# Hybrid attention/SSD layer on one core: new transfer prices and a longer search in the planner that orders the instructions

## The chip, the cores and the metric

The kernel runs on one core of a Trainium2 chip, alone. The metric is the device time of one execution in microseconds (us); smaller is better. A core has a matrix engine (PE), a vector engine (DVE), a scalar engine (ACT), a general engine (POOL) and a queue engine (SP) that issues most of the transfers (DMA). Each engine takes its instructions in the order in which they stand in its own queue and waits where an input or a buffer is not ready; the engines meet through semaphores.

## What is computed

One layer (DEPTH = 1) of a diffusion backbone on 512 latent tokens of width 1024 with 256 context tokens, in float32:

```python
cq_x, ckv_x, kr_x, z_x, xbc_x, dt_x = in_split(
    modulate(rms_norm(x, mix_pre_norm[l]), mod_x[0], mod_x[1]) @ w_in[l])
...
attn_x = latent_attention(q_nope_x, q_rope_x,
                          jnp.concatenate([k_nope_c, k_nope_x], axis=1),
                          jnp.concatenate([kr_c, k_rope_x], axis=1),
                          jnp.concatenate([v_c, v_x], axis=1))
...
y_x = ssd_output(st_xf[0], st_xf[1]) + flip(ssd_output(st_xb[0], st_xb[1]))
ssd_x = ssd_finish(y_x, xs_x, z_x, ssd_d[l], ssd_norm[l])
mix_x = jnp.concatenate([attn_x, ssd_x], axis=-1) @ w_out[l]
x = x + mod_x[2] * rms_norm(mix_x, mix_post_norm[l])
ffn_x = conv_glu(modulate(rms_norm(x, ffn_pre_norm[l]), mod_x[3], mod_x[4]),
                 w_up[l], ffn_conv_w[l], ffn_conv_b[l], w_down[l])
x = x + mod_x[5] * rms_norm(ffn_x, ffn_post_norm[l])
```

There are 16 attention heads (64 plain and 32 rotary dimensions, keys and values from a low-rank latent of width 256) and 16 SSD heads (chunks of 128 tokens, both directions).

## The kernel before

The source `build` writes the whole layer once, straight through, in an order that is easy to read. Matrices are cut into blocks of 128 rows and at most 512 columns. A float32 operand is split into a high and a low part (`split`: L498 on ACT makes the high part, L499 on DVE the difference), and a product is three PE passes over these parts. Storage in the on-chip memory is 53 blocks of 128 partitions by 1024 words; each tensor (`t4`, `t2`) takes a piece of a block. In the profile every such piece is called `block`, and every matmul result `banks`.

The stages of the profile, by the lines that dominate them:

- 0 to 150 us: modulation vectors, the norm of x, and the input projections (L686, and L759 in `gemm_T`).
- 150 to 520 us: the rest of the input projection (`rest_of_in`), the SSD (`ssd`, L1034 to L1091) and, beside them, the attention of eight pairs of heads.
- 520 to 610 us: the output projection L1326 on the rows `wout`, with the norms after it; DVE meanwhile forms more modulation values from the rows `wmod` (L587).
- 610 to 850 us: the gated MLP up (L759); 850 to 975 us: the MLP down (L1519) and the last norm.

Two places of the middle stage matter here.

*The operands of a pair of heads* (`project`, called "the projection of a pair" below). The product of the keys of both heads (in `gemm_T`, L759) lands in one bank, and is split into the block `kx[0]`: rows 0 to 63 belong to the first head, rows 64 to 127 to the second. Line L1176 copies rows 64 to 127 into `kx[1]` by DMA, block to block. Only when that copy has landed may L1181 copy the rotary keys over the same rows 64 to 127 of `kx[0]`. The queries go the same way (L1179, L1180), and the context keys `kcj` (L1176, L1182). These are 56 transfers of 128 KB and 32 of 256 KB. The first score matmul of the pair (`scores`, L1203) needs them all. `scores` goes on with a maximum on DVE (L1205), an exponential on ACT (L1207), transposes on PE (L1219) with splits (L498, L499), and the weighted sum of values (L1231), which DVE takes up in L1257.

*The norm of the key latent* (`latent("wckv", ...)` in `rest_of_in`). PE sums squares against a column of ones (L845, six products). DVE scales the sums (L847); `rsqrt` takes a power on POOL (L522) and refines it on DVE (L523, L527, L528, L529), on tensors of 128x6. PE then spreads the six values over rows (L535, six products), DVE multiplies the latent by them (L855, twice), and the next products reuse the bank (L759).

The order in which instructions stand on each engine is not that of the source. `program` traces `build` once, and `plan` decides the order and which piece gets which block. `plan` prices each instruction (`price`), finds what depends on what (`dependences`), and plays a list schedule in which transfers share one queue (`Graph.schedule`; a reader of a transfer waits `DMA_WAIT + DMA_ALONE * cost` after its turn in that queue). Then it repeats rounds: it places the pieces in blocks by the start and end times of the round before, takes an older piece's block only where that piece ends `MARGIN` (2500 ns) earlier, adds the waits that shared blocks bring, and schedules again. The plan with the smallest modelled end is kept; its order becomes the program's.

Of the kernel before, what the change touches and what calls it, by code (L numbers as in the profile page):

```python
# [86 lines left out]
UNITS, EDGE, MARGIN = 212, 180, 2500  # L87
# [7 lines left out]
class Memory:  # L95
# [3 lines left out]
    def __init__(self, pool, plan=None):  # L99
        self.pool, self.plan, self.pieces, self.blocks = pool, plan, [], {}  # L100
# [48 lines left out]
         ("Pool", "Activation"): 75, ("Pool", "DVE"): 74, ("Pool", "PE"): 149, ("Pool", "Pool"): 102}  # L149

AHEAD = 40000
DMA_START, DMA_WAIT, DMA_AHEAD, DMA_ALONE, DMA_WORDS = 650, 910, 3000, 0.8, 5000


def engine_of(x):
    return str(x.engine).split(".")[-1]
# [5 lines left out]
def price(x):  # L162

    ops = [(v.bass_ap.tensor.name, list(v.ap), v) for l in (x.outs, x.ins) for v in l if hasattr(v, "bass_ap")]
    size = lambda o: math.prod(c for _, c in o[1][1:])
    e, n = engine_of(x), max(map(size, ops))
    chip = all(not o[0].startswith("banks") for o in ops)
    kind = type(x).__name__
    if "DMA" in kind:
        words = any(len(v.bass_ap.ap) > 1 and v.bass_ap.ap[-1][0] != 1 for v in x.outs if hasattr(v, "bass_ap"))  # L170
        return DMA_WORDS if words else size(ops[0]) * ops[0][1][0][1] * 4 / 360
    if e == "PE":
        if ops[1][2].dtype == mybir.dt.float32r:
            return size(ops[1]) / (2.4 if size(ops[1]) >= 256 else 1.2) + (13 if ops[1][1][0][1] > 64 else 100)
        return max(107, size(ops[1]) / 1.2) if x.is_transpose else max(213, size(ops[1]) / 0.6)
    if "Memset" in kind:
        return 35 + 0.83 * n
    if e == "Activation":
        return 72 + (43 if chip else 0) + 93 * (len(ops) - 2) + 0.833 * n
    if e == "Pool":  # L180
        return 150 + (1.66 if any(not s for o in ops for s, c in o[1][1:] if c > 1) else 2.1) * n
    if "Reciprocal" in kind:
        return 69 + 6.25 * n
    if "TensorScalar" in kind and chip and sum(size(o) > 1 for o in ops[1:]) < 2:
        return 69 + 0.52 * n
    return (130 if len(ops) == 4 else 69) + 1.04 * n
# [192 lines left out]
        return found  # L379


def plan(ins, pieces, hints, units, rounds=16):

# [16 lines left out]
                    preds[i].update(last)  # L402
    opens, shared = {u[0] for u in users.values()}, [ports(x) for x in ins]
    _, _, start, end = Graph(preds, eng, dma, cost, share, tables, urgent, opens, shared).best()
    found = None
    for _ in range(rounds):
        held, types = [(-1, -1e9, [])] * units, [None] * (units // 4)
        inst, before = [((), -1e9)] * (units // 4), [((), -1e9)] * (units // 4)
        full, places = [set(p) for p in preds], []
        for t, (n, type_), at in pieces:  # L410
            u = users[t]
            s0, s1 = min(start[i] for i in u), max(end[i] for i in u)
            able, free, due = [], {}, {}
            for o in range(0, units, STEP[n]):
                b = o // 4
                if (o + n - 1) // 4 == b:
                    h = held[o : o + n] if types[b] == type_ else held[b * 4 : b * 4 + 4]
                    if all(v[0] < at for v in h):
                        able.append(o)
                        free[o], due[o] = max(max(v[1] for v in h), (before if types[b] == type_ else inst)[b][1]), h  # L420

            fit = [o for o in able if free[o] + MARGIN <= s0]
            fit = [o for o in fit if (o >= EDGE) == (n < 3)] or fit
            if fit:
                o = max(fit, key=lambda o: sum(v[1] for v in due[o]) / len(due[o]))
            else:
                if not able:
                    break
                o = min(able, key=free.get)
            b = o // 4  # L430
            new = types[b] != type_
            if new:
                types[b], before[b], inst[b] = type_, inst[b], ((), -1e9)
            inst[b] = (*inst[b][0], *u), max(inst[b][1], s1)
            for i in u:
                full[i].update(before[b][0])
                for v in due[o]:
                    full[i].update(v[2])
            held[o : o + n] = [(max(u), s1, u)] * n
            places.append((o, new))  # L440
        if len(places) < len(pieces):
            continue
        took, order, start, end = Graph(full, eng, dma, cost, share, tables, urgent, opens, shared).best()
        if found is None or took < found[0]:
            found = took, places, order
    return found


# [1179 lines left out]
def program(arrays, dbg_shapes=None, **kw):  # L1628

    try:  # L1630
        trace(arrays, None, dbg_shapes, **kw)
    except Traced as t:
        tiles, hints, ins = t.args
    return trace(arrays, plan(ins, tiles, hints, UNITS), dbg_shapes, **kw)
# [9 lines left out]
```

## Time and profile before

| | |
|---|---|
| median of 3 runs | 976.13 us (975.1 to 976.65) |
| the profiled execution's own time | 976.79 us |
| span of its profile, first to last instruction | 975.0 us |
| PE busy | 953.7 us (98%), 5157 records |
| DVE, ACT, POOL busy | 680.0 (70%), 504.7 (52%), 184.4 us (19%) |
| mean granted PE clock | 0.995 of full |
| DMA | 122.94 MB, mean 126 GB/s |

The profile is one execution. "Busy" of PE counts overlapping matmuls once. A wait row names an instruction group, what it waited for, the total, how often, and the longest. A window row gives, for a stretch of the span, its length and the busy time of PE, its weight loads (PEld), DVE, ACT and POOL with the number of instructions in brackets, then the granted PE clock, the share of time in which the 16 DMA engines were busy, and the GB/s that they moved. `SPq` rows are transfers that SP issues. L numbers are lines of the kernel before.

### The profile page before, as it was taken

Reading aid. Unit: us, or ns where it says so; the run is one execution under the profiler, and the core shown is the slowest. Engines: PE = TensorE matmul, PEld = TensorE weight load, DVE = VectorE, ACT = ScalarE, POOL = GpSimd, SP = SyncE. Lnnn points to the kernel's source line nnn. Section 1 sums busy time; section 2 is a strip of 40 time slices with the busy share of each in tenths; the row PEclk is TensorE's granted clock in tenths of the full one; section 3 lists DMA queues with packets and bytes.
Section 4 is the critical chain, followed back from the end, with each engine's and each line's share of the span. In section 5 each row is a group of like instructions: output and inputs, shape, how many; then the busy total and the mean of one; then the engine's idle time right before and its main releaser. Section 6 shows DMA issues by size and latency. Waiting matters only on the chain.

```text
span 975.0 us, 14205 instructions
## 1 busy us (share of the span) xinstructions
PE 953.7 (98%) x5157; PEld 813.6 (83%) x5157; DVE 680.0 (70%) x1151; ACT 504.7 (52%) x1004; POOL 184.4 (19%) x187
## 2 busy tenths in 40 slices
PE   8999999999999999999899999999999999999997
PEld 7888888888878987888798888988888888878885
DVE  6999886999999987767789966735254342695214
ACT  4554337567579787787787026633142231662001
POOL 0002202657694535111010001000000000000000
PEclk9999999999999999999899999999999999999999
DMA  9924102012321351524839876231323203347321
GB/s 349 402 94 130 44 22 82 19 66 74 95 60 55 100 153 45 133 74 110 234 138 335 248 205 216 87 108 54 140 85 132 87 33 108 98 155 241 82 84 65
DMA packets 48037, 122.94 MB, mean 126 GB/s; under 512 B 8400, under 2 KB 11552, under 8 KB 47968
## 3 DMA queue, kind: packets, MB, share of 16 engines
q1 hardware_dynamic: 45424, 120.89, 38.6%
q10 hardware_dynamic: 2544, 1.15, 0.5%
q8 instruction: 41, 0.67, 0.3%
q14 instruction: 28, 0.23, 0.1%
HBM read 99.82 MB, written 6.46 MB: 109 GB/s over the span
## 4 chain that ended last, share of the span: by engine, by line
PE 80%; DVE 5%; DMA 3%; ACT 2%; issue 1%; POOL 0%; SPq 0%; DVEq 0%; ACTq 0%; POOLq 0%
PE banks L759 38%; PE banks L1519 12%; PE banks L1326 9%; PE banks L1203 5%; PE banks L1231 3%; PE banks L1219 3%; DVE block L499 2%; DMA block<-block 2%; PE banks L1135 1%; PE banks L686 1%; PE banks L1039 1%; PE banks L1084 1%; PE banks L1076 1%; DVE smalls L1205 1%; PE banks L808 1%
## 5 line engine op out<-in xcount | busy, mean ns | idle before, releaser
L759 PE MATMUL banks<-block,block 128*128 128x512 f32 (+1 forms) x2132 | 443.2, 360 | 1.1 <-DVE block L855 1.1
L759 PEld LDWEIGHTS banks<-block,block 128*128 128x128 f32 x2132 | 358.8, 188 | 62.1 <-DVE block L855 1.4
L499 DVE TENSOR_TENSOR block<-block,block 128x512 fp32r<-128x512 f32 (+4 forms) x252 | 221.7, 904 | 121.2 <-ACT block L498 59.2
L498 ACT ACTIVATE block<-block 128x512 fp32r<-128x512 f32 (+5 forms) x252 | 181.7, 746 | 220.6 <-PE banks L759 68.9
L1519 PE MATMUL banks<-block,block 128*128 128x512 f32 x504 | 118.1, 389 | 0.2 <-ACT block L498 0.2
L1519 PEld LDWEIGHTS banks<-block,block 128*128 128x128 f32 x504 | 94.4, 188 | 20.4 <-ACT block L498 0.8
L1203 PE MATMUL banks<-block,block 128*128 128x512 f32 (+1 forms) x384 | 97.8, 359 | 7.1 <-DMA block<-in_wout_dram 3.1
L522 POOL TENSOR_TENSOR smalls<-smalls,powers 128x1 f32<-128x1 f32 (+3 forms) x16 | 12.6, 789 | 482.5 <-DVE smalls L1503 355.4
L499 DVE TENSOR_TENSOR block<-banks,block 128x256 fp32r<-128x256 f32 (+1 forms) x156 | 84.1, 556 | 14.8 <-ACT block L498 13.8
L1326 PE MATMUL banks<-block,block 128*128 128x512 f32 x384 | 91.2, 393 | 0.0
L498 ACT ACTIVATE block<-banks 128x256 fp32r<-128x256 f32 (+1 forms) x156 | 74.8, 499 | 27.9 <-PE banks L1219 14.5
L1326 PEld LDWEIGHTS banks<-block,block 128*128 128x128 f32 x384 | 71.5, 188 | 14.3
L1203 PEld LDWEIGHTS banks<-block,block 128*128 128x128 f32 x384 | 61.0, 192 | 16.0 <-ACT block L1207 4.5
L1205 DVE TENSOR_REDUCE smalls<-banks 128x1 f32<-128x768 f32 x64 | 60.9, 951 | 17.5 <-PE banks L1203 13.8
L1231 PE MATMUL banks<-block,block 128*128 128x256 f32 x384 | 70.1, 297 | 0.0
L1207 ACT ACTIVATE block<-banks,smalls 128x768 f32<-128x768 f32 x64 | 57.9, 905 | 15.4 <-DVE smalls L1205 10.7
L1219 PE MATMUL banks<-cst,block 128*128 128x128 f32 x384 | 64.3, 275 | 0.2
L587 DVE SCALAR_TENSOR_TENSOR block<-block,block 128x1024 f32<-128x1024 f32 x50 | 60.0, 1217 | 3.8 <-DMA block<-in_wmod_dram 3.6
L1231 PEld LDWEIGHTS banks<-block,block 128*128 128x128 f32 x384 | 57.8, 191 | 4.5 <-issue 0.7
L793 DVE SCALAR_TENSOR_TENSOR block<-banks,cwh,block 128x510 f32<-128x510 f32 (+3 forms) x88 | 50.9, 619 | 8.1 <-ACT block L789 7.7
L1219 PEld LDWEIGHTS banks<-cst,block 128*128 128x128 f32 x384 | 47.3, 141 | 6.9 <-DVE block L499 0.8
L686 PE MATMUL banks<-block,block 128*128 128x512 f32 x192 | 48.3, 398 | 0.6 <-ACT block L640 0.6
(228 smaller groups left out, 980.1 us busy)
## 6 DMA issues: line engine op xcount, KB each, us to landing
block<-in_wmod_dram SPq DMA_DIRECT2D x48, 512.0 KB
block<-in_wup_dram SPq DMA_DIRECT2D x44, 512.0 KB
block<-in_wdn_dram SPq DMA_DIRECT2D x44, 256.0 KB
block<-block SPq DMA_DIRECT2D x32, 256.0 KB
block<-in_wout_dram SPq DMA_DIRECT2D x16, 512.0 KB
block<-block SPq DMA_DIRECT2D x56, 128.0 KB
block<-in_wxbc_dram SPq DMA_DIRECT2D x12, 512.0 KB
block<-in_wz_dram SPq DMA_DIRECT2D x16, 256.0 KB
```

The costliest lines, as they stand in the source:

```text
L498: act(hi, src, AF.Copy)
L499: (lo_eng or V).tensor_tensor(out=lo, in0=src, in1=hi, op=ALU.subtract)
L587: V.scalar_tensor_tensor(out=junk, in0=wt, scalar=0.5, in1=vec, op0=ALU.mult, op1=ALU.mult, accum_out=acc)
L686: mm(po[i], lhsT=hx[k][:, hp, i * P : (i + 1) * P], rhs=wz[wp], start=(k == 0 and wp == 0 and hp == 0), stop=(k == KD - 1 and hp == 1))
L759: mm(po, lhsT=wf(k, pt[0]), rhs=xf(k, pt[1]), start=(k == 0 and pt == parts[0]), stop=(k == nk - 1 and pt == parts[-1]))
L1203: mm(sc[:, o : o + n], lhsT=q_[:, x_, qi * P : (qi + 1) * P], rhs=kk[:, y_, :], start=part == 0, stop=part == 2)
L1205: V.reduce_max(nm, sc[:, :T], axis=AX.X, negate=True)
L1207: act(pe, sc[:, :T], AF.Exp, bias=nm, scale=1.0, accum_out=sm_)
L1219: nc.tensor.transpose((tx if c < NX else tc_)[:, o : o + P], pe[:, s_ : s_ + P], ident)
L1231: mm(po[:, half * 256 : half * 256 + 256], lhsT=vst(c), rhs=rhs, start=(part == 0 and c == 0), stop=(part == 1 and c == NKT - 1))
L1326: mm(po[i][:, nh * 512 : nh * 512 + 512], lhsT=l[lp][:, i * P : (i + 1) * P], rhs=w[wp][:, nh * 512 : nh * 512 + 512], start=(k == 0 and l ...
L1519: mm(po[i], lhsT=l[lp][:, i * P : (i + 1) * P], rhs=w[wp], start=(k == 0 and lp == 0 and wp == 0), stop=(k == NF - 1 and lp == 1))
```

## The change

Three things in the planner; the code that is planned stays word for word, and so does the set of instructions on each engine. A transfer whose ends both lie in on-chip blocks is priced at 180 instead of 360 bytes per ns; a transfer whose destination has single words apart (the two columns that L1313 writes as rows) at 10000 instead of 5000 ns; and the search takes 56 rounds instead of 16, of which the first nine use the fixed margin as before, later ones a random margin between 0 and 5000 ns per candidate block, and every third of those starts from the times of the best plan so far.

```diff
-DMA_START, DMA_WAIT, DMA_AHEAD, DMA_ALONE, DMA_WORDS = 650, 910, 3000, 0.8, 5000
+DMA_START, DMA_WAIT, DMA_AHEAD, DMA_ALONE, DMA_WORDS = 650, 910, 3000, 0.8, 10000
...
-        return DMA_WORDS if words else size(ops[0]) * ops[0][1][0][1] * 4 / 360
+        inside = all(isinstance(o[2].bass_ap.tensor, tile.Tile) for o in ops)
+        return DMA_WORDS if words else size(ops[0]) * ops[0][1][0][1] * 4 / (180 if inside else 360)
...
-def plan(ins, pieces, hints, units, rounds=16):
+def plan(ins, pieces, hints, units, rounds=56):
...
-    found = None
-    for _ in range(rounds):
+    found, rng = None, np.random.default_rng(0)
+    for n_ in range(rounds):
+        if n_ > 8 and n_ % 3 == 0:
+            start, end = kept_
...
-            fit = [o for o in able if free[o] + MARGIN <= s0]
+            fit = [o for o in able if free[o] + (MARGIN if n_ < 9 else rng.uniform(0, 2 * MARGIN)) <= s0]
...
         if found is None or took < found[0]:
-            found = took, places, order
+            found, kept_ = (took, places, order), (start, end)
```

The new plan moves instructions nearly everywhere from 50 us on; the first instructions (on PE 175) and the last ones (on PE 84) stand as before. Lines after `plan` have numbers higher by 3 in the changed kernel: L1176 is L1179 there. Three places follow in which the prediction's terms lie.

First place, SP, the last pair of heads (its keys `kx[0]` are block_716 before and block_206 after; `in_wmod_dram` and `in_wout_dram` are rows of 512 KB from the main memory). Before:

```order
L490 DMA block_444_2675<-in_wout_dram 128x1024
L1180 DMA block_567_3382<-block_198_1365 32x1024
L490 DMA block_665_4053<-in_wout_dram 128x1024
L1176 DMA block_756_4626<-block_716_4364 64x1024
L490 DMA block_824_5069<-in_wmod_dram 128x1024
L490 DMA block_808_4999<-in_wmod_dram 128x1024
L490 DMA block_835_5109<-in_wmod_dram 128x1024
L1176 DMA block_26_231<-block_153_880 64x512
L1181 DMA block_716_4364<-block_198_1365 64x1024
```

After:

```order
L493 DMA block_819_5076<-in_wout_dram 128x1024
L493 DMA block_613_3749<-in_wmod_dram 128x1024
L1182 DMA block_671_4087<-block_706_4352 32x1024
L1179 DMA block_756_4637<-block_206_1420 64x1024
L1183 DMA block_671_4087<-block_198_1359 32x1024
L493 DMA block_810_5040<-in_wout_dram 128x1024
L1184 DMA block_206_1420<-block_198_1359 64x1024
```

Between the copy out of `kx[0]` and the copy into it stood three loads from the main memory and one copy; now one load and one copy stand there.

Second place, PE, the norm of the key latent. After, the end of the stretch from the sums of squares (L848, five rows above the first of these) to the spread values:

```order
L762 MATMUL banks<-block_47_360,block_306_2000 128x512
L762 MATMUL banks<-block_47_360,block_307_2001 128x512
L762 MATMUL banks<-block_116_672,block_306_2000 128x256 x2
L762 MATMUL banks<-block_41_318,block_306_2000 128x512
L762 MATMUL banks<-block_116_672,block_307_2001 128x256
L762 MATMUL banks<-block_116_672,block_306_2000 128x256
L762 MATMUL banks<-block_41_318,block_306_2000 128x512
L762 MATMUL banks<-block_116_672,block_306_2000 128x256
L762 MATMUL banks<-block_116_672,block_307_2001 128x256
L762 MATMUL banks<-block_41_318,block_307_2001 128x512
L762 MATMUL banks<-block_117_673,block_306_2000 128x256
L538 MATMUL banks<-cst,smalls 128x128 x6
```

From the last of the sums to the first spreading product PE had 42 matmuls before, 23 of them 512 and 19 of them 256 wide; now it has 18, of which 11 are 512 and 7 are 256 wide.

Third place, DVE, the same norm. Before:

```order
L847 TENSOR_SCALAR smalls<-banks 128x6
L523 TENSOR_SCALAR smalls<-smalls 128x6
L1086 TENSOR_TENSOR block_7_88<-banks,block_7_88 128x512
L527 TENSOR_TENSOR smalls<-smalls 128x6
L1065 TENSOR_TENSOR block_178_1131<-block_178_1131,block_11_116 128x256
L528 TENSOR_TENSOR smalls<-smalls 128x6
L1065 TENSOR_TENSOR block_178_1131<-block_178_1131,block_11_116 128x256
L529 SCALAR_TENSOR_TENSOR smalls<-smalls 128x6
```

After:

```order
L850 TENSOR_SCALAR smalls<-banks 128x6
L526 TENSOR_SCALAR smalls<-smalls 128x6
L530 TENSOR_TENSOR smalls<-smalls 128x6
L1068 TENSOR_TENSOR block_279_1812<-block_279_1812,block_209_1432 128x256
L531 TENSOR_TENSOR smalls<-smalls 128x6
L1068 TENSOR_TENSOR block_279_1812<-block_279_1812,block_209_1432 128x256
L532 SCALAR_TENSOR_TENSOR smalls<-smalls 128x6
```

The instruction L1086 no longer stands among the chain's own five; the two L1065 (now L1068) still do.

## The prediction

> **What bounds the kernel now.** I read the page's totals first, then PE's waits, then windows by stage.
>
> ```profile
> span 975.0 us, 14205 instructions
> PE 953.7 (98%) x5157; PEld 813.6 (83%) x5157; DVE 680.0 (70%) x1151; ACT 504.7 (52%) x1004; POOL 184.4 (19%) x187
> PE banks L1203 <- DMA block<-in_wout_dram: 3.1, 1, 3.1
> PE banks L1203 <- ACT block L1207: 1.6, 3, 0.9
> PE banks L1203 <- DMA block<-block: 1.6, 2, 1.2
> PE banks L759 <- DVE block L855: 1.1, 1, 1.1
> PE banks L1203 <- issue: 0.7, 1, 0.7
> 225.00:375.00 150.00, 145.06 (x866) 123.56 (x864) 133.08 (x223) 118.41 (x299) 86.53 (x81) 1.00 0.33 86
> 375.00:475.00 100.00, 98.60 (x659) 86.97 (x658) 79.20 (x137) 78.74 (x176) 26.43 (x27) 1.00 0.43 113
> 475.00:525.00 50.00, 46.71 (x307) 41.86 (x306) 42.29 (x70) 39.67 (x78) 3.85 (x3) 0.93 0.64 218
> 525.00:965.00 440.00, 439.78 (x2089) 369.00 (x2088) 227.26 (x361) 146.67 (x230) 10.31 (x13) 1.00 0.40 130
> ```
>
> PE bounds it: it stands still for 975.0 - 953.7 = 21.3 us. The matmuls are the same after the change, so a plan can win only idle time and lost clock. From 525 to 965 us there is nothing to win (0.22 us idle). The first and the last instructions keep their order, so the idle time at both ends stays. What is left lies between 225 and 525 us: 4.9 + 1.4 + 3.3 = 9.6 us of idle, and in the window 475 to 525 a clock of 0.93. There DVE is the second bound: 133.08 of 150 us is 89% busy.
>
> **The largest stall.** It is in the last pair of heads.
>
> ```profile
> 469.60 0.50 SPq L1176 DMA_DIRECT2D block<-block  x1
> 470.15 3.15 SPq L490 DMA_DIRECT2D block<-in_wmod_dram  x3
> 476.06 0.50 SPq L1181 DMA_DIRECT2D block<-block  x1
> 482.55 1.62 PE L1203 MATMUL banks<-block,block 128*128 128x512 f32 x3 [3.13 <-DMA block<-in_wout_dram]
> 479.40:482.50 3.10, 0.02 (x1) 0.00 (x0) 0.65 (x1) 2.41 (x6) 0.00 (x0) 0.84 1.02 257
> 482.50:487.00 4.50, 4.45 (x15) 3.92 (x15) 3.98 (x5) 1.06 (x1) 0.00 (x0) 0.50 0.64 183
> 391.63 0.48 SPq L1176 DMA_DIRECT2D block<-block  x1
> 395.23 0.55 SPq L1181 DMA_DIRECT2D block<-block  x1
> 400.10 0.94 PE L1203 MATMUL banks<-block,block 128*128 128x512 f32 x3 [1.25 <-DMA block<-block]
> ```
>
> The wait row names a load of `wout`, which no score matmul reads. In the code this L1203 reads `kx[0]`, which L1181 fills, and L1181 waits for L1176. In the fifth pair, the last three rows, the scores began 400.10 - 391.63 = 8.5 us after L1176 was issued; here 482.55 - 469.60 = 13.0 us, with three loads of `wmod` between the copies. After 3.1 us without a matmul the granted clock is 0.50 for 4.5 us, so another 4.45 / 2 = 2.2 us is lost.
>
> **The change, part by part.**
>
> *The price of block-to-block copies.* Is twice the price nearer the truth? In the first row below only such copies were in flight, in the second only loads from the main memory.
>
> ```profile
> 265.00:268.25 3.25, 3.25 (x21) 2.82 (x20) 2.03 (x3) 2.73 (x6) 3.25 (x3) 1.00 0.89 204
> 25.00:45.00 20.00, 20.00 (x117) 17.47 (x117) 19.12 (x42) 11.08 (x20) 0.00 (x0) 1.00 1.04 401
> 863.30 104.35 PE banks L1519 x459
> 446.35 1.20 PE banks L1231 x10
> 453.29 1.09 PE banks L1219 x10
> ```
>
> Copies move 204 GB/s with the DMA engines 89% busy, loads 401: half, as the new price has it. What the plan makes of it shows in PE's order. A 512-wide matmul takes 104.35 / 459 = 0.227 us, a 256-wide one 0.12, a transpose 0.11. Between the key product of a pair and the first score that reads the copied rows stood, in the fifth pair, 64 matmuls worth 8.9 us, now 87 worth 12.1; over the sixteen such places (plain and context keys of eight pairs) the mean goes from 9.5 to 11.9 us, and 15 of 16 grow. The fifth pair's wait of 1.2 us and the second's 0.4 us (cover 10.2, now 14.4) are gone by that: the 1.6 us of the wait row. In the last pair the cover hardly grows (12.4 to 12.9 us), but one load instead of three stands between the copies. With the 8.5 us of the fifth pair the operands would be there at 469.6 + 8.5 = 478.1, before the 479.4 at which PE came. So 3.1 + 2.2 us go. Bounds: nothing, if the load that still stands there does the same harm, and all 5.3.
>
> [...]
>
> *What is late next in the last pair.* With PE 5.3 us earlier there, DVE has to keep up. It had 50 - 42.29 = 7.7 us free in that window, about 2.5 of it inside the stall. The new order also puts three modulation products (L587) before the end of the attention that stood after it.
>
> ```profile
> L587 DVE SCALAR_TENSOR_TENSOR block<-block,block 128x1024 f32<-128x1024 f32 x50 | 60.0, 1217 | 3.8 <-DMA block<-in_wmod_dram 3.6
> ```
>
> Three are 3 x 1.217 = 3.7 us against 5.2 us free, so they fit by the sum, though not each in its place. Bounds: 0, and the whole 5.3 given back. I take 1.5, nearer the lower end since the work fits.
>
> *The norm of the key latent.* This place gets worse.
>
> ```profile
> 220.87 2.26 POOL L1090 TENSOR_TENSOR block<-block 128x512 f32<-128x512 f32 x1
> 221.33 1.39 PE L845 MATMUL banks<-ones,block 128*128 128x1 f32 x12
> 223.61 0.15 DVE L847 TENSOR_SCALAR smalls<-banks 128x6 f32<-128x6 f32 x1
> 223.79 1.07 DVE L523 TENSOR_SCALAR smalls<-smalls 128x6 f32<-128x6 f32 x1
> 224.80 1.33 POOL L522 TENSOR_TENSOR smalls<-smalls,powers 128x6 f32<-128x6 f32 x1
> 226.16 0.69 DVE L527 TENSOR_TENSOR smalls<-smalls 128x6 f32<-128x6 f32 x1 [0.60 <-POOL smalls L522]
> 227.73 1.00 DVE L528 TENSOR_TENSOR smalls<-smalls 128x6 f32<-128x6 f32 x1
> 228.99 0.70 DVE L529 SCALAR_TENSOR_TENSOR smalls<-smalls 128x6 f32<-128x6 f32 x1
> 230.22 1.50 PE L535 MATMUL banks<-cst,smalls 128*128 128x128 f32 x12
> 234.99 2.33 PE L759 MATMUL banks<-block,block 128*128 128x512 f32 x9 [1.07 <-DVE block L855]
> ```
>
> The chain ran from the end of L845 at 222.7 to the end of L529 at 229.7: 7.0 us, covered by 42 matmuls (23 x 0.227 + 19 x 0.12 = 7.5). Now 18 cover it: 11 x 0.227 + 7 x 0.12 = 3.3. Without L1086, which left the chain, and without the wait for a busy POOL, I put the chain at some 5.7 us, so PE waits 2.4 us at L535. The next hand-over gains: 12 matmuls stood between L535 and L759, now 22 (10 x 0.227 + 12 x 0.12 = 3.7 us), while L759 could start 235.0 - 231.7 = 3.3 us after L535; the 1.1 us there go. Net 2.4 - 1.1 = +1.3. Lower bound +0.2 (both L1065 out of the chain). Upper: the full 7.0, 3.7 - 1.1 = 2.6, and if the clock halves as after the other stall, 2.2 more: 4.8.
>
> *The price of word-wise transfers.*
>
> ```profile
> 554.59 0.39 ACTq L1313 DMA_DIRECT2D mod_rows<-mod  x1
> 567.86 0.35 ACTq L1315 DMA_DIRECT2D block<-mod_rows  x1
> ```
>
> ACT, which issues both, could read back only 13.3 us after the write, so 10 us is nearer than 5. PE is busy throughout (0.22 us idle in 440), so this costs and gains nothing; without that cover the 13.3 us would stand on ACT. *The 40 more rounds and random margins* have no row of their own: they move all other waits. I leave the rest of the 9.6 us as it is and put +/- 2.5, half of the 4.9 us between 225 and 375, into the range.
>
> **The sum.** -1.6 - 5.3 + 1.5 + 1.3 = -4.1 us against the profiled 976.79: 972.7. That execution lies 0.66 above the median, so beside the median it is 976.13 - 4.1 = 972.0.
>
> **The rivals.** A difference under 0.2% (1.95 us: 974.2 to 978.1) can't be told from no change.
>
> - *DVE takes the stall's place*: at 89% busy from 225 to 375 it has little room, against it stands the sum of free time above. All 5.3 come back: 976.13 - 1.6 - 5.3 + 5.3 + 1.3 = 975.8.
> - *The change does not do what it says in the last pair*: one 512 KB load still stands between the copies, the cover grew by 0.5 us only. Then only 1.6 is won and 1.3 lost, and DVE owes nothing: 975.8. Against it: the three loads that took DMA time are gone from there. [...]
> - *The norm's stall, slower*: POOL's power stands behind an L1090 now, and small operations of one shape took from 0.15 to 1.07 us in the rows. A power late by the whole L1090 (2.3) and both L1065 half a us longer each (the rows leave room of 0.9 and 0.3 us for them) make the chain 7.0 + 2.3 + 1.0 = 10.3 us; the wait is then 7.0 and with the halved clock 9.2, which is 8.1 net: 972.0 - 1.3 + 8.1 = 978.8. It decides from a chain of 9.6 us on.
>
> **How the numbers follow.** Forecast 0.56 (972.0, with its own range 968 to 974.2): the covers are counted, and the two copies' rows show what they cost. DVE's return 0.14, no effect in the last pair 0.12 (both within 0.2%), the norm or some other new wait of its kind 0.18. Faster 0.56, same 0.26, slower 0.18. Low end: the gains alone with half of the open idle time, 976.13 - 6.9 - 2.5 = 966.7; high end: the last pair's stall stays and the norm costs its upper bound, 976.13 - 1.6 + 4.8 = 979.3. I take 966.5 to 979.
>
> **What would show it.** Right: no wait of L1206 (L1203 before) for a transfer over 0.5 us, a clock of 1.00 between 450 and 525 us, and a new wait of L538 (L535 before) for L532 of 1 to 3 us near 230 us. Wrong: a wait of L1206 at the last pair again, PE idle in 475 to 525 still near 3.3 us with DVE as the releaser, or a stretch with a clock of 0.5 after L538. The whole would be wrong if 225 to 375 us, where I count on no change but the norm, gained or lost more than 2.5 us.

## The result, and the profile after

| | before | after |
|---|---|---|
| median of 4 runs each | 976.39 us (975.1 to 977.04) | 970.58 us (969.63 to 970.97) |
| the profiled execution's own time | 976.79 us | 969.63 us |
| span of its profile | 975.0 us | 967.5 us |

The ratio is 0.9941, interval 0.9923 to 0.9958: 5.8 us less, between 4.1 and 7.5. The profiled execution of after is the shortest of its four runs, so the two profiles differ by more, 7.2 us. Forecast were 972.0 us and a range of 966.5 to 979.

The page's totals, then PE's waits (what waited, for what, total, times, longest), then the windows, with the columns of the prediction:

```profile
span 967.5 us, 14200 instructions
PE 950.1 (98%) x5157; PEld 809.9 (84%) x5157; DVE 679.8 (70%) x1151; ACT 506.0 (52%) x1004; POOL 193.2 (20%) x187
PE banks L1206 <- ACT block L1210: 2.0, 3, 1.0
PE banks L620 <- DVE block L614: 1.9, 1, 1.9
PE banks L681 <- POOL block L649: 1.3, 1, 1.3
PE banks L538 <- DVE smalls L532: 1.0, 2, 0.6
PE banks L1234 <- DVE block L1260: 0.6, 2, 0.5
225.00:375.00 150.00, 146.22 (x864) 123.43 (x863) 138.66 (x233) 119.72 (x298) 91.04 (x87) 1.00 0.34 90
375.00:475.00 100.00, 99.03 (x674) 87.81 (x672) 78.99 (x133) 80.43 (x177) 21.58 (x23) 1.00 0.46 122
475.00:525.00 50.00, 49.84 (x327) 44.40 (x325) 47.71 (x75) 39.55 (x76) 4.40 (x3) 1.00 0.75 254
```

No wait of L1206 (L1203 before) for a transfer is left; there were 3.1 and 1.6 us. From 475 to 525 us PE's idle time fell from 3.29 to 50 - 49.84 = 0.16 us and the granted clock rose from 0.93 to 1.00. The other windows gave 1.2 us (4.94 to 3.78 idle in the first) and 0.4 us (1.40 to 0.97). Idle between 225 and 525 us went from 9.63 to 4.91 us, 4.7 less. Over the whole span, 7.5 us shorter, PE's idle time fell by 3.9 us (975.0 - 953.7 = 21.3, then 967.5 - 950.1 = 17.4) and its busy time by 3.6 us. Most of the latter is the half clock: before, it lasted beyond the 4.5 us that the prediction looked at, over 5.85 us of matmuls (a clock of 0.50 from 482.55 to 488.40 us, PE busy throughout), which is 5.85 / 2 = 2.9 us instead of 2.2.

### The profile page after: what moved, and what is told of

It is laid out like the page before. It is cut to its first block, busy times and chain, and to the rows that moved or that the text cites. A ratio compares the mean times of both kernels' runs of the same rounds, so it can differ in the third digit from the quotient of the medians.

```text
span 967.5 us, 14200 instructions
## 1 busy us (share of the span) xinstructions
PE 950.1 (98%) x5157; PEld 809.9 (84%) x5157; DVE 679.8 (70%) x1151; ACT 506.0 (52%) x1004; POOL 193.2 (20%) x187
## 3 DMA queue, kind: packets, MB, share of 16 engines
HBM read 99.82 MB, written 6.46 MB: 110 GB/s over the span
## 4 chain that ended last, share of the span: by engine, by line
PE 57%; DVE 3%; ACT 1%; issue 1%; DMA 1%; POOL 0%; DVEq 0%; ACTq 0%; POOLq 0%
PE banks L762 26%; PE banks L1522 12%; PE banks L1329 8%; PE banks L1206 3%; PE banks L1234 3%; PE banks L1222 2%; DVE block L502 1%; PE banks L1138 1%; DMA block<-in_wmod_dram 1%; DVE smalls L1208 1%; PE banks L1111 0%; PE banks L1079 0%; ACT block L1428 0%; DVE block L1260 0%; ACT block L1385 0%
## 5 line engine op out<-in xcount | busy, mean ns | idle before, releaser
L762 PE MATMUL banks<-block,block 128*128 128x512 f32 (+1 forms) x2132 | 448.4, 361 | 0.4 <-DVE block L502 0.2
L762 PEld LDWEIGHTS banks<-block,block 128*128 128x128 f32 x2132 | 360.2, 189 | 60.6 <-DVE block L796 0.9
L502 DVE TENSOR_TENSOR block<-block,block 128x512 fp32r<-128x512 f32 (+4 forms) x252 | 224.7, 917 | 101.2 <-ACT block L501 34.7
L501 ACT ACTIVATE block<-block 128x512 fp32r<-128x512 f32 (+4 forms) x252 | 180.7, 746 | 184.6 <-PE banks L762 55.0
L1206 PE MATMUL banks<-block,block 128*128 128x512 f32 (+1 forms) x384 | 95.7, 354 | 2.3 <-ACT block L1210 2.0
L502 DVE TENSOR_TENSOR block<-banks,block 128x256 fp32r<-128x256 f32 (+1 forms) x156 | 83.2, 556 | 13.9 <-ACT block L501 12.6
L1206 PEld LDWEIGHTS banks<-block,block 128*128 128x128 f32 x384 | 60.2, 189 | 10.3 <-ACT block L1210 4.9
```

What stands on the lines that cost most here:

```text
L501: act(hi, src, AF.Copy)
L502: (lo_eng or V).tensor_tensor(out=lo, in0=src, in1=hi, op=ALU.subtract)
L762: mm(po, lhsT=wf(k, pt[0]), rhs=xf(k, pt[1]), start=(k == 0 and pt == parts[0]), stop=(k == nk - 1 and pt == parts[-1]))
L1206: mm(sc[:, o : o + n], lhsT=q_[:, x_, qi * P : (qi + 1) * P], rhs=kk[:, y_, :], start=part == 0, stop=part == 2)
```

## The experiments

The prediction named one stall as the place of the gain and the new price of copies as its cause. The rival is that the price matters little and the longer search just finds a better plan. Twelve kernels bear on it. "Modelled end" is the planner's own estimate of a plan in the source, not a time of the chip; "cover" is the mean of the sixteen places between a key product and the score that reads its copy, worked out as in the prediction from the plans' orders, which are not printed here. Each ratio is against runs of before on the same chip in the same set.

| kernel | modelled end | cover us | PE's waits for copies | median us | ratio (interval) |
|---|---|---|---|---|---|
| after (profiles above) | 971.0 | 11.9 | none | 970.58 | 0.9941 (0.9923 to 0.9958) |
| e1_prices | 974.9 | 11.6 | none | 971.31 | 0.9960 (0.9948 to 0.9973) |
| e3_fixed_margin | 969.0 | 12.8 | none | 967.99 | 0.9921 (0.9907 to 0.9934) |
| e5_other_seed | 974.9 | 11.9 | none | 971.96 | 0.9956 (0.9940 to 0.9972) |
| e6_margin_1000 | 966.9 | 11.4 | none | 966.16 | 0.9896 (0.9879 to 0.9914) |
| e8_inside_price | 974.7 | 12.6 | none | 973.01 | 0.9961 (0.9949 to 0.9973) |
| before | 972.2 | 9.5 | 3 in all, 4.7 us | 975.3 to 976.6 | 1 |
| e2_search | 966.5 | 9.3 | 1, 0.6 us | 966.47 | 0.9908 (0.9895 to 0.9922) |
| e4_ten_rounds | 972.2 | 8.7 | 3, 2.4 us | 976.28 | 1.0008 (0.9993 to 1.0022) |
| e7_words_price | 974.6 | 10.0 | 1, 0.8 us | 971.94 | 0.9948 (0.9933 to 0.9963) |
| e9_old_prices_margin_1000 | 965.8 | 8.9 | 3, 1.6 us | 971.57 | 0.9948 (0.9936 to 0.9961) |

The upper six price copies inside at 180 bytes per ns, the lower five at 360.

### The stall of the last pair, taken out of the plan of before

Three kernels keep before's plan and move only transfers on SP. The first puts the plain keys' second copy, and the context keys' first, ahead of the three modulation loads:

```diff
-    return trace(arrays, plan(ins, tiles, hints, UNITS), dbg_shapes, **kw)
+    found = plan(ins, tiles, hints, UNITS)
+    sp, to = found[2]["SP"], [x.outs[0].bass_ap.tensor.name.split("_")[0] for x in ins]
+    at = [k for k, i in enumerate(sp) if to[i] in ("piece824", "piece808", "piece835")]
+    sw = max(k for k, i in enumerate(sp) if to[i] == "piece755")
...
+    sp[at[0] : sw + 1] = [sp[sw], sp[sw - 1]] + sp[at[0] : at[0] + 3]
+    return trace(arrays, found, dbg_shapes, **kw)
```

> The plan of before, with one place of SP's order edited: in the last pair of heads the copy into the first key block (L1181) and the copy of the context keys (L1176) stand directly behind the first copy (L1176), ahead of the three modulation loads instead of behind them. All other orders are those of before. Theory one (the change's gain is the last pair's stall): the stall of 3.1 us and the half clock after it go, 976.4 - 5.3 = 971.1 us, the clock between 475 and 525 us is 1.00, and this single move of three loads is worth nearly the whole change. Rival (DVE is late next there, since the attention's vector work is the second bound): PE waits for DVE instead, at least half comes back, 973.7 to 976. Rival two (the search's plan as a whole is better, the stall only its symptom): under 2 us gained, above 974.4.

Measured: 977.94 us, ratio 1.0023 (1.0011 to 1.0034), slower. Its last pair, SP's issues and PE:

```profile
469.59 0.50 SPq L1176 DMA_DIRECT2D block<-block  x1
475.34 0.51 SPq L1181 DMA_DIRECT2D block<-block  x1
476.54 1.56 SPq L490 DMA_DIRECT2D block<-in_wmod_dram  x3
479.61 0.50 SPq L1182 DMA_DIRECT2D block<-block  x1
478.88 0.95 PE L1203 MATMUL banks<-block,block 128*128 128x512 f32 x3
487.62 1.01 PE L1203 MATMUL banks<-block,block 128*128 128x256 f32 x3 [4.73 <-DMA block<-block]
```

The plain scores now started at 478.88 without a wait, against 482.55 before. But the context keys' second copy L1182 was issued behind the loads, and PE waited 4.73 us for it. The three loads between the plain copies had indeed delayed the second of them: before, PE began 6.5 us after L1181 was issued (476.06), here 3.5 us after, without a wait. The first copy they had hardly delayed: L1181 waits for it and could go only at 475.34, 5.75 us after L1176, with nothing between them any more (6.46 us before). So the stall had moved to the next copy in the queue. The second kernel puts all the key copies first:

```diff
...
+    last = max(k for k, i in enumerate(sp) if to[i] == "piece757")
+    copies = [i for i in sp[at[0] : last + 1] if to[i] in ("piece755", "piece757", "piece758")]
...
+    sp[at[0] : last + 1] = copies + [i for i in sp[at[0] : last + 1] if i not in copies]
```

> The plan of before, SP's order edited in the last pair: all four copies of the keys (both L1176, then L1181 and L1182) stand ahead of the three modulation loads, the wout load, the transfer of the shares and the next modulation load that stood among them. In d1_swap only the plain keys' copies went ahead of the loads, and the stall moved to the context keys' copy L1182, which then had five loads ahead of it. Theory (the stall is the transfer queue: load bytes ahead of whichever key copy lands last): no score of the last pair waits for a transfer over 0.5 us, the clock between 475 and 525 us is 1.00, and 5.3 us go: ratio to before 0.9946, 970.0 us beside a before of 975.3. Rival (something else is late there, a load that the out-projection or DVE needs, and takes the stall's place): at least half comes back, ratio 0.997 to 1.000.

Measured: 976.7 us, ratio 1.0000 (0.9984 to 1.0016). No gain, and the rival had it right. ACT and PE there:

```profile
479.97 0.47 SPq L490 DMA_DIRECT2D block<-in_wout_dram  x1
487.13 1.06 ACT L498 ACTIVATE block<-block 128x1024 fp32r<-128x1024 f32 x1 [4.17 <-DMA block<-in_wout_dram]
489.00 0.74 PE L1231 MATMUL banks<-block,block 128*128 128x256 f32 x4 [3.35 <-ACT block L498]
```

Now the load of `wout` was the late one: issued at 479.97 behind the three loads, taken up at 487.13. ACT waited 4.17 us for it with the attention's splits queued behind, and PE waited 3.35 us for ACT. PE's stall did not bring the half clock here: the first two rows below are 480 to 490 us in before and in this kernel, with a granted clock of 0.66 and of 1.00. The queue was full at that place in before, and is no longer in after (both 470 to 480 us, third and fourth row):

```profile
480.00:490.00 10.00, 7.45 (x34) 6.74 (x35) 5.18 (x8) 4.78 (x10) 1.39 (x2) 0.66 0.71 211
480.00:490.00 10.00, 6.50 (x42) 5.26 (x41) 7.25 (x11) 5.83 (x12) 0.00 (x0) 1.00 0.79 288
470.00:480.00 10.00, 9.40 (x76) 8.75 (x74) 7.83 (x14) 9.21 (x19) 0.00 (x0) 1.00 1.02 302
470.00:480.00 10.00, 9.74 (x70) 8.47 (x68) 9.14 (x18) 8.76 (x19) 0.00 (x0) 1.00 0.71 212
509.78 1.22 DVE L587 SCALAR_TENSOR_TENSOR block<-block,block 128x1024 f32<-128x1024 f32 x1
```

In before the DMA engines were busy all the time there (share 1.02). The last row, DVE's first L587 after 430 us in before, shows when the three loads issued at 470 were needed: they were read from 509.8 us on. The third kernel puts the three copies first, and these loads and a fourth one like them last:

```diff
...
+    part = sp[at[0] : last + 1]
+    copies = [i for i in part if to[i] in ("piece755", "piece757", "piece758")]
+    mod = [i for i in part if to[i] in ("piece824", "piece808", "piece835", "piece806")]
...
+    sp[at[0] : last + 1] = copies + [i for i in part if i not in copies + mod] + mod
```

> The plan of before, SP's order in the last pair edited a third time: the four copies of the keys first, then the wout load and the shares, and the four modulation loads last. DVE reads those four only from 509 us on, 30 us after they are issued; ACT and DVE read the wout load at 482 us. In d1_swap the transfer that came late was the context keys' copy (PE waited 4.7 us), in d2_copies_first the wout load (ACT waited 4.2 us for it and PE 3.4 us for ACT); each time the load bytes ahead of it made it late. Theory (the stall is worth 5.3 us, and it is the modulation loads that make whatever stands behind them late): neither waits now, the clock between 475 and 525 us is 1.00, ratio to before 0.9946 (970.5 beside 975.8). Rival (the plan is late at that place by its vector work, whatever the queue does): ratio 0.998 to 1.001, with PE waiting for DVE or ACT there.

Measured: 972.31 us, ratio 0.9955 (0.9941 to 0.9968), 4.4 us faster (3.1 to 5.8). Its window, and the wait that was left in it:

```profile
475.00:525.00 50.00, 48.70 (x319) 42.90 (x318) 47.56 (x74) 42.60 (x82) 5.77 (x4) 1.00 0.78 264
490.60 0.66 PE L1219 MATMUL banks<-cst,block 128*128 128x128 f32 x3 [1.02 <-DVE block L499]
```

So, in the plan of before, the stall is worth 4.4 us, with about 1 that DVE takes back already in it, and five transfers in another place on one queue (four loads to the end, one copy ahead of the `wout` load) bring three quarters of what the whole change brings. What made a transfer late in these plans was what stood ahead of it in the queue. The plan of after has a like order: five modulation loads in a row stand behind the pair's last copy (L1185), and between it and L1184 one, at 474.62:

```profile
470.69 0.49 SPq L1184 DMA_DIRECT2D block<-block  x1
474.62 0.34 SPq L493 DMA_DIRECT2D block<-in_wmod_dram  x1
478.25 0.54 SPq L1185 DMA_DIRECT2D block<-block  x1
478.83 5.33 SPq L493 DMA_DIRECT2D block<-in_wmod_dram  x5
```

The three kernels agree in this: in d1_swap and d2_copies_first a transfer that SP had issued behind the loads was late (PE waited 4.7 us for a copy, ACT 4.2 us for `wout`), and in d3_mod_last, with the key copies and that `wout` load ahead of the four loads, PE waited for no transfer from 470 to 530 us; its one wait there is the 1.02 us for DVE.

### Prices alone, search alone

> Both new prices (inside copies 180 bytes per ns, word-wise transfers 10000 ns) with the search of before: 16 rounds, fixed margin. Its planner's own modelled end is 974.9 us, that of the full change 971.0, so the search adds 3.9 us by the planner. In its order the covers of the copies are as long as after the change (mean of the sixteen places 11.6 us; before 9.5, after 11.9), and in the last pair no load stands between the two copies. Theory one (prices remove the waits for copies): 1.6 + 5.3 us go, 976.4 - 6.9 = 969.5, with 2.5 us to either side for the other waits that a new plan moves: 967 to 972. Rival (the longer search is what gains): the planner's 3.9 us are missing, 970.6 + 3.9 = 974.5.

To the kernel before:

```diff
-DMA_START, DMA_WAIT, DMA_AHEAD, DMA_ALONE, DMA_WORDS = 650, 910, 3000, 0.8, 5000
+DMA_START, DMA_WAIT, DMA_AHEAD, DMA_ALONE, DMA_WORDS = 650, 910, 3000, 0.8, 10000
...
-        return DMA_WORDS if words else size(ops[0]) * ops[0][1][0][1] * 4 / 360
+        inside = all(isinstance(o[2].bass_ap.tensor, tile.Tile) for o in ops)
+        return DMA_WORDS if words else size(ops[0]) * ops[0][1][0][1] * 4 / (180 if inside else 360)
```

Measured: 971.31 us, 0.9960. Inside the first theory's range, though nearer its upper end; 3.2 us better than the rival's 974.5.

> The new search alone (56 rounds, random margins, restarts), with the old prices. By the planner's own modelled end it is 5.6 us better than before (966.5 against 972.2, both under the old prices). The covers of the copies stay as short as before (mean 9.3 us); in the last pair one load stands between the copies, but the cover there is 11.1 us for the plain keys and 8.4 for the context keys. Theory one (the price is what matters): the short covers make PE wait for copies at three to six places, 1 to 5 us in all, and the last pair waits again (0.5 to 2 us) but with less or no half clock: 972 to 976. Rival (the search is what gains): 976.4 - 5.6 = 970.8 or less.

To the full change:

```diff
-DMA_START, DMA_WAIT, DMA_AHEAD, DMA_ALONE, DMA_WORDS = 650, 910, 3000, 0.8, 10000
+DMA_START, DMA_WAIT, DMA_AHEAD, DMA_ALONE, DMA_WORDS = 650, 910, 3000, 0.8, 5000
...
-        return DMA_WORDS if words else size(ops[0]) * ops[0][1][0][1] * 4 / (180 if inside else 360)
+        return DMA_WORDS if words else size(ops[0]) * ops[0][1][0][1] * 4 / 360
```

Measured: 966.47 us, 0.9908. The rival was right by far, and the kernel with the old prices is faster than the full change. The waits that I expected from its short covers came to one (first row, of PE's waits), and PE is idle for only 1.13 us from 225 to 375 us:

```profile
PE banks L1206 <- DMA block<-block: 0.6, 1, 0.6
225.00:375.00 150.00, 148.87 (x887) 126.63 (x886) 138.04 (x230) 121.68 (x306) 88.90 (x84) 1.00 0.34 90
475.00:525.00 50.00, 49.54 (x318) 43.42 (x317) 47.34 (x75) 39.72 (x76) 5.97 (x5) 1.00 0.78 271
```

The two parts don't add up: prices -0.40%, search -0.92%, both -0.59%. Each draws another plan, and the stall of the last pair is missing from all of them.

### Is it the draw?

Five kernels vary the draw. The first leaves the random part out but keeps 56 rounds:

```diff
-        if n_ > 8 and n_ % 3 == 0:
+        if False:
...
-            fit = [o for o in able if free[o] + (MARGIN if n_ < 9 else rng.uniform(0, 2 * MARGIN)) <= s0]
+            fit = [o for o in able if free[o] + MARGIN <= s0]
```

> The new prices and 56 rounds, but the margin stays at 2500 ns and no round starts from the best plan: the random part of the search left out. Its planner's modelled end is 969.0 us, 2.0 under that of the full change (971.0), reached in round 40. Covers are long (mean 12.8 us), no load stands between the copies of the last pair. Theory one: no wait for copies, as after, and what differs is only the small waits, 968 to 972, about the time of the full change (970.6). Rival (the planner's modelled end tells the time to within 1 us once the prices are right): 970.6 - 2.0 = 968.6.

Measured: 967.99 us, 0.9921. At the edge of the first theory's range, and within 1 us of the rival's 968.6. The intervals of this ratio and of the full change's overlap (0.9907 to 0.9934, 0.9923 to 0.9958), so that it is faster is likely and not shown; random margins and restarts, at any rate, aren't what gains. With them seed 0 reached 971.0 by the model, without them 969.0. The rounds do gain: e1_prices is this same search ended after 16 rounds, and 40 more took it from 974.9 to 969.0 by the model and from 971.31 to 967.99 us on the chip.

> The kernel before with 10 instead of 16 rounds, old prices. Its best plan is that of round 10, modelled end 972.2 us, within 0.1 of the plan that before keeps (round 13, 972.2): the planner can't tell the two apart. Covers of the copies are the shortest of all (mean 8.7 us), but in the last pair no load stands between the plain keys' copies. Theory one (before is one plan with a stall that the planner doesn't see; a tie without that stall is faster by about it): 971 to 973. Rival (old prices make short covers, and short covers cost time): waits for copies at four or more of the sixteen places, 975 or slower.

```diff
-def plan(ins, pieces, hints, units, rounds=16):
+def plan(ins, pieces, hints, units, rounds=10):
```

Measured: 976.28 us, 1.0008. The rival was right in the time: the tie by the model is a tie on the chip, without the last pair's stall but with waits for copies elsewhere (first row) and DVE late at four places (second row):

```profile
PE banks L1203 <- DMA block<-block: 2.4, 3, 1.0
PE banks L1039 <- DVE block L1044: 2.2, 4, 0.7
```

> The full change, with the random numbers of seed 1 instead of 0. No random round finds a better plan than round 8, which comes ahead of the random part: modelled end 974.9 us, 4.0 more than the full change and no better than the prices alone (974.9). If the planner's modelled end told the time to 1 us: 974.5. If any plan with the new prices is as good, since its covers are long (mean 11.9): 970.6. The prices alone measured 971.3 with the same modelled end, so I expect 971 to 973; two modulation loads stand between the copies of the last pair, with 13.1 us of cover, so a wait of up to 1 us there.

```diff
-    found, rng = None, np.random.default_rng(0)
+    found, rng = None, np.random.default_rng(1)
```

Measured: 971.96 us, 0.9956, as expected; with another seed the long search adds nothing to the prices.

> The kernel before with only the price of word-wise transfers changed (10000 ns), 16 rounds. Modelled end 974.6 us. Covers are nearly those of before (mean 10.0 us; before 9.5, both prices 11.6), no load between the plain keys' copies of the last pair. Theory (it is the price of inside copies that gains; old inside prices give 3.5 to 4 us more than the planner's modelled end, as in before and e4_ten_rounds): 975 to 979, no gain. Rival (any new draw of the plan gains, the inside price has no part): 970 to 973.

```diff
-DMA_START, DMA_WAIT, DMA_AHEAD, DMA_ALONE, DMA_WORDS = 650, 910, 3000, 0.8, 5000
+DMA_START, DMA_WAIT, DMA_AHEAD, DMA_ALONE, DMA_WORDS = 650, 910, 3000, 0.8, 10000
```

Measured: 971.94 us, 0.9948. My theory fell here: with the old price for copies and 16 rounds, a plan came out that is as good as those of 16 rounds with the new one. The word-wise price concerns two transfers that are hidden, and yet its draw is 4.7 us faster than before.

> The kernel before with only the price of inside copies changed (180 bytes per ns), 16 rounds. Modelled end 974.7 us, the same as e7_words_price; covers long (mean 12.6 us). Theory (the inside price alone is the prices' part): as e1_prices and e5_other_seed (971.3 and 972.0 with a modelled end of 974.9), 970.5 to 972. Rival (no part of it, or both prices are needed): 974 to 977.

```diff
-        return DMA_WORDS if words else size(ops[0]) * ops[0][1][0][1] * 4 / 360
+        inside = all(isinstance(o[2].bass_ap.tensor, tile.Tile) for o in ops)
+        return DMA_WORDS if words else size(ops[0]) * ops[0][1][0][1] * 4 / (180 if inside else 360)
```

Measured: 973.01 us, 0.9961; no wait for a copy in it, 1 us above the theory's range and 1 us below the rival's.

### A version that beats both

> The new prices, 80 rounds, no random part, and a fixed margin of 1000 instead of 2500 ns for taking over a block. Modelled end 966.9 us, 4.1 under the full change and 2.1 under e3_fixed_margin (968.0 us measured, modelled 969.0). If the margin's safety isn't needed, the time follows the model: 966 to 967. Rival (the margin covers transfers and blocks that come late): PE and the loads wait for blocks at several places, 969 to 973.

To e3_fixed_margin:

```diff
-UNITS, EDGE, MARGIN = 212, 180, 2500
+UNITS, EDGE, MARGIN = 212, 180, 1000
...
-def plan(ins, pieces, hints, units, rounds=56):
+def plan(ins, pieces, hints, units, rounds=80):
```

Measured: 966.16 us, 0.9896 (0.9879 to 0.9914), the fastest of all medians; against e2_search's 966.47 the difference can't be told. It has half the idle time of after from 225 to 375 us (1.74 against 3.78 us), and next to none in the two windows behind:

```profile
225.00:375.00 150.00, 148.26 (x891) 127.19 (x891) 134.30 (x227) 122.47 (x311) 87.98 (x83) 1.00 0.34 90
375.00:475.00 100.00, 99.87 (x683) 89.26 (x682) 83.86 (x140) 82.47 (x183) 28.16 (x27) 1.00 0.41 110
475.00:525.00 50.00, 49.97 (x316) 44.08 (x315) 46.18 (x74) 39.51 (x74) 4.64 (x4) 1.00 0.81 290
```

The same margin and rounds with the two old prices of e2_search:

> The old prices with 80 rounds, no random part and a fixed margin of 1000 ns: modelled end 965.8 us, the lowest of all, 0.7 under e2_search and 1.1 under e6_margin_1000, which measured 966.5 and 966.2. If an old-price plan runs 3.5 to 4 us over its modelled end, as before and e4_ten_rounds did, 969.5; if e2_search is the rule (no excess), 965.8; I expect 968, since its price is too short but the search is long.

Measured: 971.57 us, 0.9948, 5.8 over the lowest modelled end of all, from waits for a copy at three places and for what hangs on ACT:

```profile
PE banks L1206 <- ACT block L1210: 2.2, 4, 1.4
PE banks L1522 <- ACT block L501: 2.1, 2, 1.1
PE banks L1206 <- DMA block<-block: 1.6, 3, 0.9
375.00:475.00 100.00, 96.74 (x653) 85.62 (x651) 78.95 (x134) 78.98 (x174) 26.09 (x26) 1.00 0.39 105
```

### What the table says together

With the inside price at 180 no plan of six has a wait of PE for a copy (the lists go down to 0.2 us); at 360 each of five has one to three. That is what the price does, and it is shown. But outside the last pair these waits come to 0.6 to 2.4 us, and plans differ by more than that for other reasons. Three pairs of searches differ in the prices alone: with 16 rounds the new prices are faster (971.3 against 975.3 to 976.6), with the search of the full change the old ones (966.5 against 970.6), with 80 rounds and a margin of 1000 the new ones (966.2 against 971.6). What else differs is how far the modelled end can be trusted. With both new prices the five plans run in the order of their modelled ends (966.9, 969.0, 971.0, 974.9, 974.9 by the model; 966.2, 968.0, 970.6, 971.3, 972.0 on the chip), 0.4 to 3.6 us under them, though two of these ends tie and e8_inside_price, with the inside price alone, ran behind both of that tie (974.7 by the model, 973.0). At 360 the model tells less (965.8, 966.5, 972.2, 972.2, 974.6 by the model; 971.6, 966.5, 976.4, 976.3, 971.9 on the chip): from 2.7 us under to 5.8 over; the two lowest ends beat before, but the lowest of all ran 5.1 us behind the next. I read this so, which eleven plans suggest and don't show: the new price lets the search choose by something that holds on the chip. Whether e2_search's 966.5 was luck under a wrong price stays open, since only one plan of that search ran.

## Why the prediction was right, point by point

- *Copies' waits, -1.6 us.* Right: those waits are gone, as the longer covers said, and the table shows the inside price as their cause.
- *The last pair, -5.3 us.* Right in effect: both the 3.1 us and the half clock are gone. By d3_mod_last the removal alone is worth 4.4 us in the plan of before. The reason was half right. The loads between the two copies did delay the second one (6.5 us from issue to scores before, 3.5 in d1_swap), but taking them from between is not enough: d1_swap is slower, d2_copies_first has all copies first and gains nothing. The queue was full (a share of 1.02), in part with loads that nobody needed for 30 us more, and in d1_swap and d2_copies_first a transfer behind them was late (PE waited 4.7 us for a copy, ACT 4.2 us for `wout`). So the one load that still stands between the copies in after need do no harm: five modulation loads come behind the pair's last copy there. The low share there (0.71) is no proof by itself, since d2_copies_first shows 0.75 from 470 to 480 us and PE stalls there from 485.6 on. The half clock is the less certain part: in before it cost 2.9 us rather than the 2.2 of the sum, and in d2_copies_first PE stood for 3.35 us without it.
- *DVE late next, +1.5 us.* Too high for after: 0.16 us idle in that window, with DVE busy 47.71 of 50 us. In d3_mod_last it is 1.02 us, so the term exists in the old plan; the new one had room for it.
- *The key latent's norm, +1.3 us.* The step that failed: the sign is wrong. I counted the covers right, but put the chain at 5.7 us, and it took 223.2 to 227.1, 3.9 us; the wait of 1 to 3 us at L538 that was to show me right came to 0.42:

```profile
221.84 1.39 PE L848 MATMUL banks<-ones,block 128*128 128x1 f32 x12
223.35 0.16 DVE L850 TENSOR_SCALAR smalls<-banks 128x6 f32<-128x6 f32 x1 [0.91 <-PE banks L848]
223.54 0.17 DVE L526 TENSOR_SCALAR smalls<-smalls 128x6 f32<-128x6 f32 x1
223.59 1.33 POOL L525 TENSOR_TENSOR smalls<-smalls,powers 128x6 f32<-128x6 f32 x1
224.88 1.44 POOL L1067 TENSOR_TENSOR block<-block 128x256 f32<-128x256 f32 x2
224.95 0.69 DVE L530 TENSOR_TENSOR smalls<-smalls 128x6 f32<-128x6 f32 x1 [1.23 <-POOL smalls L525]
226.38 1.41 POOL L911 MEMSET block<- 32x512 f32 x2
226.52 0.15 DVE L531 TENSOR_TENSOR smalls<-smalls 128x6 f32<-128x6 f32 x1
226.93 0.15 DVE L532 SCALAR_TENSOR_TENSOR smalls<-smalls 128x6 f32<-128x6 f32 x1
227.14 1.60 PE L538 MATMUL banks<-cst,smalls 128*128 128x128 f32 x12 [0.42 <-DVE smalls L532]
```

DVE took the sums 0.1 us after PE had them, where it had been 0.9 us late behind a split (L499); POOL took the power 0.1 us after its input, where it had come 1.0 us late; and the three small operations after it took 0.69 + 0.15 + 0.15 us, where they had taken 0.69 + 1.00 + 0.70. PE waited 0.42 us, and L762's 1.1 us for DVE went as counted: -0.7 us instead of +1.3. The rival that grew from this place, 978.8 us, never had its chain of 9.6 us. It was right that the power stands behind the long POOL operation (L1093 in after), but that one ended at 223.57, just as the power's input came at 223.51; the prediction had no row for that, so in this part the outcome was luck.

- *The open rest, +/- 2.5 us.* Idle time from 225 to 375 us fell by 1.2 us, of which 0.7 is the norm's; inside the bound. Against it, PE began worse: the wait of L620 for L614 at 12 us is 1.9 us, after 1.3. That is no work of the plan, since those first instructions stand as before, and the same wait took 1.0 us in d1_swap.
- *The rivals.* DVE or a transfer taking the stall's place did not happen to after. It did happen in d1_swap and d2_copies_first, so it was a real rival, with transfers rather than DVE behind it.

In sum -4.1 us were forecast and -5.8 measured. By the two profiles the terms are -1.6 for the copies, -3.1 - 2.9 for the last pair and its clock, 0 for DVE's return and -0.7 for the norm: -8.3, against 7.5 between the spans. The norm and DVE's return were thus 3.5 us too dear together, and the half clock 0.7 too small. PE's start takes 0.6 of the 0.8 us between -8.3 and -7.5 back. The profiled run of before lies 0.4 us above its median and that of after 0.95 below, so the medians differ by 5.8 only; which terms are smaller in a usual run is not settled. That 972.0 came within 1.5 us of the median is in part luck: two errors of 3.5 us together stood in it.

What the prediction didn't see is that this plan is one draw among many. The search as written reached 970.6; the eight others that were tried with 16 rounds or more span 966.2 to 973.0. Before, also drawn in 16 rounds, and its tie e4_ten_rounds are the two slowest of the plans that a search drew, at 976, so a part of any gain over before may be that its draw was a poor one.

## What to carry to other kernels

Where a planner searches by a model, first make its prices right where the trace shows waits that the model doesn't have, then search; a lower modelled end under a wrong price can't be relied on (965.8 modelled and 971.6 measured, but also 966.5 and 966.5). A late copy behind a full transfer queue was mended here by what was taken out of the queue ahead of everything urgent, so look for the loads whose reader is far away, and move those, not only the copies: the copies alone gained nothing here, copies and loads together 4.4 us. And before a gain is put down to an edit of a scheduler, run two or three other draws: here an edit of the price of two hidden transfers moved the time by 4.7 us.

## What was not expected of the hardware

- *A small DVE operation of one shape took from 0.15 to 1.07 us, and the time went with what POOL did beside it.* In after, L531 took 0.15 us beside a MEMSET of POOL, and L530 0.69 us beside POOL's L1067, whose first of two ends when L530 ends (224.88 + 1.44 / 2 = 225.60 and 224.95 + 0.69 = 225.64). In before the 1.07 us of L523 ended with POOL's L1080 (224.86 and 224.84) and the 1.00 us of L528 with its L1070 (228.73 and 228.72):

```profile
223.10 1.74 POOL L1080 TENSOR_TENSOR block<-block,block 128x512 f32<-128x512 f32 x1
227.49 1.23 POOL L1070 TENSOR_TENSOR block<-block,block 128x512 f32<-128x512 f32 x1
```

L847, which reads `banks`, took 0.15 us beside the same L1080. The rows show that the times went together, not why.

- *Copies within the memory moved 204 GB/s, loads 401.* Both rates are readings of before (265 to 268.25 us with the DMA engines' share at 0.89, 25 to 45 us at 1.04), and the planner of before priced both kinds at 360 bytes per ns. The copies in flight from 265 us on move 32 or 64 rows each. So the new price of 180 is nearer to what these copies moved.
- *Before varies more than some other plans.* Beside the experiments, 23 runs of before took 972.4 to 979.0 us and 12 of e4_ten_rounds 973.7 to 978.6, while six of e5_other_seed took 971.5 to 972.4 and five of e6_margin_1000 965.4 to 966.9. The two that spread by 5 to 7 us have waits of PE for copies (4.7 and 2.4 us), the other two none, but that is not the reason by itself: d1_swap has 5.9 us of them, and its nine runs took 976.9 to 978.7. The granted clock goes with a part of it: of all 47 runs of before, the 23 with a mean clock of 0.996 or more have a median of 974.9 us, the 24 with less 976.6.
